# A two-layer decoder trunk: the row of reciprocal norms by two float32r products, a whole copy of the low-rank block, and 32 columns more in the planner's product estimate

## The chip, the cores and the metric

The kernel runs on one core of one Trainium2 chip. The metric is the device time of one execution in microseconds; before the change it is 489.7 us, the median of three runs that lie between 489.56 and 489.83 us. The engines are called as the profile calls them: PE (TensorE's products) and PEld (its weight loads), DVE (VectorE), ACT (ScalarE), POOL (GpSimd) and SP (SyncE, which issues transfers).

## The reference

Two layers of a decoder trunk on 512 tokens of width 1024, all in float32. Cut to what matters:

```python
def hybrid_layer(x, ...):
    h = rmsnorm(x, norm_g)                       # (512, 1024)
    p = h @ w_in                                 # (512, 3488), split by columns
    cq, ckv, kr, g_a, c_h, c_b, c_c, g_b, sg_u, sg_v, g_c, mq, mk, mv, g_d = split(p)
    # A: latent attention, 4 heads. The low-rank block is cq (256), ckv (128), kr (32)
    q  = rmsnorm(cq, mla_q_norm_g) @ mla_w_uq
    kv = rmsnorm(ckv, mla_kv_norm_g) @ mla_w_ukv
    k_rope = rope(rmsnorm(kr, mla_k_rope_g))
    o_a = causal softmax attention on q, [k_nope, k_rope], v
    o_b = c_b * short_conv(c_c * c_h)            # B
    o_c = sg_u * (causal mixing of layernorm(sg_v))   # C
    o_d = attention in blocks, 4 heads, on mq, mk, mv   # D
    y = concat(o_a * silu(g_a), o_b * silu(g_b), o_c * silu(g_c), o_d * silu(g_d))
    return y @ w_out
x = x + hybrid_layer(x, ...)                     # twice
```

## The kernel before

**Products.** Each float32 operand of a large product is split into a high and a low float32r part, and each product is done as three float32r products (high by high, high by low, low by high) that add up in one PSUM bank; `mm3` writes these three. `ScalarE` usually makes a high part (`whi_...`, `hTh...`, `cTh`, `ph..`) and VectorE the low part (`wlo_...`, `hTl`, `cTl`, `pl..`). Transposes and one more product, the one this change is about, run in float32. Some of the large products are made in the seven-product form of Strassen and Winograd (`t1` to `t4`, `p1` to `p4`, `b11` and so on), whose sums of weights are made by accumulating transfers on POOL's queue (`t_sums`, from `TS0` on).

**The planner.** No loop of the kernel fixes the order of the instructions. Every chain of work is a Python generator, and `Order.run` resumes them by due time and priority. It keeps a time `now`, which is the planned time of PE, and a clock for each of ACT (`A`), VectorE (`V`), POOL (`G`) and the transfers (`D`). `Chain.pe` puts a product into PE's queue once its inputs are due (plus `PEMARGIN`, 80 ns) and moves `now` by the estimate that it is given, which is `cost(n)` for a product of n columns. `Chain.act`, `Chain.dve` and `Chain.pool` move their engine's clock by an estimate from the size. Choices between ACT and VectorE (the copies `ct`, the scaling of the softmax rows `pa` and `pd`, the high parts of weights, the means by head) go by whose clock is behind. So each engine gets one fixed order of instructions, and at run time it waits only where a semaphore makes it wait. Some chains start at written times: the mixing of group C at `MIXT`, the row of norms at `ROWT`, the columns of gains at `COLT`, the sums of weights at `TS0`, all in planned nanoseconds.

**Banks and buffers.** PSUM's eight banks are handed out by three sets of slots: `accS` (three, for the large products), `trS` (two, for transposes) and `sS` (three). A slot that nobody has put back makes the chain that wants it wait in the plan, and makes the instruction wait at run time. `t2S` hands out eleven SBUF buffers of 128x512.

**The start of layer 0.** The rows of x are not normalized before the first product. x is transposed (`xT`), split (`hTh`, `hTl`) and multiplied as it is, and the reciprocal norm, rstd, is put in afterwards. `x_stats` gathers the mean squares; at `ROWT` POOL raises them to the power -1/2 into `xv[:, RR, :]`, 128 partitions by four token blocks. Groups whose products come out with the features on the partitions need rstd along a row: `x_row` makes a 128x512 matrix `rd` of four diagonals on POOL, multiplies ones by it in float32 on PE (`rrow`), and ACT writes half of the row and its square to `rh`, which the gates and the convolution read later.

**The low-rank block.** `c_first` makes the products `cq0` to `cq3` of the four token blocks, 416 columns each, in the three `accS` banks and one `sS` bank. For each block `low_chain` copies the first 384 columns to `ct`, transposes them (`cT`), splits the transpose (`cTh`, `cTl`) and makes `q` and `kv`. Beside it `low_stats` takes three sums of squares and a copy of the last 32 columns (`krt`) from the same bank. The bank is put back when both are done, that is after five reads, and the next large products (`sq`, columns of `sg_v` and `mq`) take these banks. In layer 1 the same two functions run on blocks that take the three `accS` banks in turn.

**The heads.** For each head of groups A and D: scores (`sa..`, `sd..`), one pass on VectorE that scales and masks a block and finds its extreme (`pa..`, `pd..`), exponentials on ACT, a reciprocal of the four sums (`mna`, `mnd`), a scaling of each block on ACT or VectorE, transposes on PE (`pTa`, `pTd`), a split (`ph..`, `pl..`) and the products with the values (`oa`, `od`). PE fills the time between these steps with the large products of the groups.

The lines of the profile carry helpers' lines: L178 is the line where `Chain._emit` issues (all of ACT's, VectorE's and POOL's planned instructions), L208 is the line where `Chain.pe` issues. So groups are told apart by the names of their tiles.

Of the kernel before, what the change touches and what calls it, by code (L numbers as in the profile page):

```python
# [11 lines left out]
F32 = mybir.dt.float32  # L12
F32R = mybir.dt.float32r
I32 = mybir.dt.int32
AF = mybir.ActivationFunctionType
ALU = mybir.AluOpType
AX = mybir.AxisListType

P = 128
S = 512  # L20
NT = S // P
# [11 lines left out]
WSLACK = 0.0  # L33
AHEAD, URGENT, VSLACK = 4, 2, 300.0
NWARM, FILL, FILLEND = 6, 0.9, 15000.0
MIXT, MIXLAG, ROWT, COLT = 42000.0, 2000.0, 36000.0, 17500.0
KSPLIT, HMEAN = 6, 0.0
PAIRS = {}
LOPRIO = -5
# [8 lines left out]
SEQ1 = ['p11', 'ga0', 'p21', 'p3', 'ga1', 'p4', 'p2', 'ch0', 'p1', 'p22', 'cc0', 'gd0', 'gd1', 'su0', 'gc0', 'cb0', 'gb0', 'ch1', 'cc1', 'cb1', 'gb1', 'su1', 'gc1']  # L48
K0, K1, KK = (2, 3, 0, 1), (4, 5, 6, 7), (0, 2, 3, 1)
ZPROD = ("b11", "t3", "b21", "t4", "t2", "t1", "b22")  # L50
TS0 = 62000.0
TAIL = ((0, 256), (256, 512))

C_CQ, C_KV, C_GA, C_CH, C_CB, C_CC, C_GB = 0, 256, 416, 672, 928, 1184, 1440
# [96 lines left out]
def run_now(gen):  # L151

    try:
        next(gen)
    except StopIteration as e:
        return [e.value]
# [57 lines left out]


def cost(n):
    return max(n / 2.4, 107.0) + 2.0


@with_exitstack  # L220
def hybrid_trunk(ctx: ExitStack, tc: tile.TileContext, x, positions, norm_g, w_c, w_f, w_t, w_o, mla_q_norm_g,
# [3 lines left out]
    V, A, G, PE = nc.vector, nc.scalar, nc.gpsimd, nc.tensor  # L225

    cst = ctx.enter_context(tc.tile_pool(name="cst", bufs=1))
# [14 lines left out]
    o = Order()  # L242
# [5 lines left out]
    t2S = Slots(o, NT2, lambda name, dt=F32: t2p.tile([P, S], dt, tag="t2", name=name))  # L248
# [254 lines left out]
    def shared(slots, n):  # L503

        left = [n]

        def put(ch):
            left[0] -= 1
            if left[0] == 0:
                slots.put(ch)  # L510
        return put
# [4 lines left out]
    ident = cst.tile([P, P], F32, name="ident")  # L516
# [21 lines left out]
    one_box = run_now(zzS.get(Chain(o), "ones", F32R))  # L538
# [137 lines left out]
    for l in range(DEPTH):  # L676
        L = Layer()
# [38 lines left out]
    def pow_rstd(ch, dst, src, n):  # L716
        return ch.pow(G.tensor_tensor, dst, src, nhalf[:, :n], op=ALU.pow)
# [5 lines left out]
    xhi, xlo = ([Event() for _ in range(KT)] for _ in range(2))  # L723
    xsum = cst.tile([P, NT, KT // 2], F32, name="xsum")
    xv = cst.tile([P, 4, NT], F32, name="xv")
    v_ev, r_ev, rh_ev = Event(), Event(), Event()
    rh_box, rh_put = [], shared(hS, 14)
    RV, RR, RE, REE = range(4)

    def rv(i, t):  # L730
        return xv[:, i, t:t + 1]
# [33 lines left out]
    def x_stats():  # L765
        ch = Chain(o)
        for kp in range(KT // 2):
            yield from ch.wait(xk_ev[2 * kp + 1])
            for t in range(NT):
                yield from ch.act(A.activation, junk[:, 0:2 * P], xk[kp][:, t, :], AF.Square, scale=D ** -0.5,  # L770
                                  accum_out=xsum[:, t, kp:kp + 1])
            c2 = Chain(o, ch.t)
            yield from c2.wait(xk_tr[2 * kp + 1])
            v4S.put(c2)
        yield from ch.dve(V.tensor_reduce, xv[:, RV, :], xsum, axis=AX.X, op=ALU.add)
        yield from ch.dve(V.tensor_scalar, xv[:, RV, :], xv[:, RV, :], 1.0, EPS, op0=ALU.mult, op1=ALU.add)
        t0 = ch.t
        for i, f in ((RE, EPS), (REE, EPS * EPS)):
            yield from ch.dve(V.tensor_scalar, xv[:, i, :], xv[:, RV, :], f, None, op0=ALU.mult)
        o.set(v_ev, ch.t)  # L780
        c2 = Chain(o, max(t0, ROWT))
        yield from pow_rstd(c2, xv[:, RR, :], xv[:, RV, :], NT)
        o.set(r_ev, c2.t)

    def x_row():

        ch = Chain(o)
        yield from ch.wait(r_ev)
        d = yield from t2S.get(ch, "rd")
        yield from ch.pool(G.tensor_tensor, d.rearrange("p (t c) -> p t c", t=NT),  # L790
                           ident.unsqueeze(1).to_broadcast([P, NT, P]),
                           xv[:, RR, :].unsqueeze(2).to_broadcast([P, NT, P]), op=ALU.mult)
        tp = yield from trS.get(ch, "rrow")
        yield from ch.pe(4 * cost(S), PE.matmul, tp, one_box[0][:, 0:P].bitcast(F32), d, start=True, stop=True)
        zz_put(ch)
        t2S.put(ch)
        rh_box.append((yield from hS.get(ch, "rh")))
        yield from ch.act(A.activation, rh_box[0][:, 0:S], tp, AF.Copy, scale=0.5)
        yield from ch.act(A.activation, rh_box[0][:, S:2 * S], tp, AF.Square, scale=0.5)
        trS.put(ch)  # L800
        o.set(rh_ev, ch.t)
# [149 lines left out]


    def low_stats(L, t, a, t0, done):
        ch = Chain(o, t0)
        ssq, krt = L.ssq, L.krt
        ct = L.ct[t]
        for i, (c0, c1) in enumerate(((384, 416), (256, 384), (0, 256))):
            yield from ch.act(A.activation, junk[:, :c1 - c0], a[:, c0:c1], AF.Square, scale=(c1 - c0) ** -0.5,
                              accum_out=ssq[:, t, 2 - i:3 - i])
        yield from ch.act(A.activation, krt[:, t, :], a[:, 384:416], AF.Copy)  # L960
        done(ch)
        m = sm.tile([P, 8], F32, tag="ms", name=f"ms{t}_{L.l}")
        e1, e2 = EPS, EPS * EPS
        if L.l == 0:
            yield from ch.wait(v_ev)
            e1, e2 = rv(RE, t), rv(REE, t)
        yield from ch.dve(V.tensor_scalar, m[:, 0:2], ssq[:, t, 1:3], 1.0, e1, op0=ALU.mult, op1=ALU.add)
        yield from ch.dve(V.tensor_scalar, L.e2[:, t, :], ssq[:, t, 0:2], EPS, e2, op0=ALU.mult, op1=ALU.add)
        yield from pow_rstd(ch, m[:, 4:6], m[:, 0:2], 2)
        L.ms[t] = m  # L970
        o.set(L.stat[t], ch.t)
        yield from ch.dve(V.scalar_tensor_tensor, krt[:, t, :], in0=krt[:, t, :], scalar=m[:, 5:6], in1=L.gr,
                          op0=ALU.mult, op1=ALU.mult)
        L.kr_left -= 1
        if L.kr_left:
            return
        yield from ch.wait(rope_ev)
        yield from rope(ch, krt, 16, cosT, sinT, f"k{L.l}")
        yield from ch.wait(L.QK_ev)
        yield from ch.pool(G.tensor_copy, L.K[:, :, :, 64:96], krt.unsqueeze(2).to_broadcast([P, NT, 4, 32]))  # L980
        o.set(L.kr_ev, ch.t)

    def low_chain(L, t, a, t0, slots):
        ch = Chain(o, t0)
        l = L.l
        done = shared(slots, 2)
        ct = yield from t2S.get(ch, f"ct{t}_{l}")
        L.ct[t] = ct
        o.spawn(low_stats(L, t, a, t0, done))
        if o.clk["A"] < o.clk["V"]:  # L990
            yield from ch.act(A.activation, ct[:, :384], a[:, :384], AF.Copy)
        else:
            yield from ch.dve(V.tensor_copy, ct[:, :384], a[:, :384])
        done(ch)
        tp = yield from trS.get(ch, f"cT{t}_{l}")
        for k in range(3):
            yield from ch.pe(109.0, PE.transpose, tp[:, k * P:(k + 1) * P], ct[:, k * P:(k + 1) * P], ident)
        t2S.put(ch)
        c_h = yield from t2S.get(ch, f"cTh{t}_{l}", F32R)
        c_l = yield from t2S.get(ch, f"cTl{t}_{l}", F32R)  # L1000
        yield from split2(ch, c_h[:, :384], c_l[:, :384], tp[:, :384])
        trS.put(ch)
        q_ps = yield from sS.get(ch, f"q{t}_{l}")
        for k in range(2):
            uq_h, uq_l = yield from unit(ch, f"uq_{l}", k)
            yield from mm3(ch, 384, q_ps[:, :384], c_h[:, k * P:(k + 1) * P], c_l[:, k * P:(k + 1) * P],
                           uq_h[:, k, :], uq_l[:, k, :], k == 0, k == 1)
        o.spawn(q_chain(L, t, q_ps, ch.t))
        uk_h, uk_l = yield from unit(ch, f"ukv_{l}")
        kv_ps = yield from sS.get(ch, f"kv{t}_{l}")  # L1010
        yield from mm3(ch, 512, kv_ps, c_h[:, 256:384], c_l[:, 256:384], uk_h[:, 0, :], uk_l[:, 0, :], True, True)
        t2S.put(ch)
        t2S.put(ch)
        L.up_left -= 1
        if L.up_left == 0:
            units[f"uq_{l}"].slots.put(ch)
            units[f"ukv_{l}"].slots.put(ch)
        yield from kv_chain(L, t, kv_ps, ch.t)
# [668 lines left out]
    def main():  # L1687
        m = Chain(o)
# [207 lines left out]
        early_put(m)  # L1896
        for L in layers:
            l = L.l
            L.ct, L.ms, L.up_left = {}, {}, NT
            L.kr_ev, L.kr_left = Event(), NT  # L1900
            L.vn_alloc = Event()
            L.md_alloc = {"mq": Event(), "mk": Event()}
# [5 lines left out]
            for t in L.torder if l else ():  # L1908
                a = yield from accS.get(m, f"cq{t}_{l}")
# [10 lines left out]
            for n in SEQ1 if L.stok else SEQ:  # L1920
# [6 lines left out]
                elif n in TOKS:  # L1927
                    us = []
                    for ts in PAIRS.get((n, l), range(NT)):
                        ts = ts if isinstance(ts, tuple) else (ts,)  # L1930
                        a = {}
# [15 lines left out]
                else:  # L1947
                    a = yield from accS.get(m, f"{n}_{l}")
# [60 lines left out]
    def start():  # L2009
# [5 lines left out]
        wp = yield from sS.get(cw, "warm")  # L2015
        ones = one_box[0][:, 0:P].bitcast(F32)
        V.memset(ones, 1.0)
        A.activation(xsum[:, 0, 0:1], ones[:, 0:1], AF.Square, scale=D ** -0.5)
        o.fill = lambda: PE.matmul(wp[:, 0:P], ones, ones, start=True, stop=True)
        for _ in range(NWARM):  # L2020
# [29 lines left out]
        o.spawn(main(), None, 10)  # L2050
    o.spawn(t_sums((0, z_src, "t", "b"), *((l, p_src, "p", "p") for l in STOK)), TS0, 4)
    o.spawn(start())
# [51 lines left out]
```

## Time and profile before

| | |
|---|---|
| median of three runs | 489.7 us |
| lowest, highest | 489.56, 489.83 us |
| the profiled execution | 489.73 us |
| its span, first to last instruction | 488.0 us |
| PE busy | 481.6 us, 99% of the span |
| DVE busy | 400.9 us, 82% |
| ACT busy | 329.9 us, 68% |
| POOL busy | 104.4 us, 21% |
| granted PE clock | 0.999 |

The 1.7 us between the span and the time of the same execution lie around the first and the last instruction. PE is busy in nearly all of the span, and its granted clock is full, so the time is read as PE's work plus the places where PE waits. A record of PE has a start and a modelled end, and the ends overlap the next starts; what a product takes from PE is read from one start to the next.

### The profile page before, as it was taken

How to read it: one execution, taken by the hardware profiler on the slowest of the kernel's cores; microseconds unless marked ns; L12 is line 12 of the kernel's file. 1: busy time of each engine (PE TensorE's matmuls, PEld its weight loads, DVE VectorE, ACT ScalarE, POOL GpSimd, SP SyncE). 2: the span in 40 equal slices, each digit the busy share in tenths (PEclk: the TensorE clock that was granted, in tenths of full speed). 3: DMA queues.
4: the chain of work that ended last, by engine and by line, in shares of the span. 5: the costliest groups of instructions: out<-in, count | busy, mean ns of one | idle time of the engine just before them, and what ended most of it. 6: DMA issues, size and time to landing. Idle time of an engine off the chain costs nothing.

```text
span 488.0 us, 7509 instructions
## 1 busy us (share of the span) xinstructions
PE 481.6 (99%) x2432; PEld 408.9 (84%) x2432; DVE 400.9 (82%) x893; ACT 329.9 (68%) x898; POOL 104.4 (21%) x172
## 2 busy tenths in 40 slices
PE   9999999999999999999999999999999999999997
PEld 7988888888887888888889988888888888888786
DVE  3698487668987899789998688979788998997993
ACT  5896837677546766457667788769675687666650
POOL 7855330710051210000031013620402200000000
PEclk9999999999999999999999999999999999999999
DMA  8742335897499888596574186786832744427762
GB/s 263 249 135 78 124 128 218 225 197 162 151 330 240 208 217 218 188 343 224 199 239 145 65 290 250 165 246 177 209 131 85 153 136 146 173 66 258 253 242 89
DMA packets 41904, 92.89 MB, mean 190 GB/s; under 512 B 7158, under 2 KB 23048, under 8 KB 41480
## 3 DMA queue, kind: packets, MB, share of 16 engines
q1 hardware_dynamic: 29168, 79.82, 47.3%
q0 software_dynamic: 12672, 12.58, 16.7%
q8 instruction: 19, 0.31, 0.2%
q14 instruction: 21, 0.17, 0.1%
q10 hardware_dynamic: 24, 0.01, 0.0%
HBM read 84.53 MB, written 33.03 MB: 241 GB/s over the span
## 4 chain that ended last, share of the span: by engine, by line
PE 91%; DVE 3%; ACT 2%; DMA 2%; SPq 1%; issue 1%; ACTq 0%
PE oy L208 6%; PE cq L208 6%; PE kv L208 6%; PE gb L208 5%; PE su L208 5%; PE cc L208 5%; PE sq L208 5%; PE gc L208 5%; PE ch L208 5%; PE ga L208 4%; PE oz L208 4%; PE cb L208 4%; PE py L208 3%; PE ox L208 3%; PE sa L208 3%; PE gd L208 3%
## 5 line engine op out<-in xcount | busy, mean ns | idle before, releaser
L178 ACT ACTIVATE pa<-pa,mna 128x128 f32<-128x128 f32 (+3 forms) x53 | 27.8, 554 | 5.6 <-DVE mna L178 5.5
L178 ACT ACTIVATE pd<-pd,mnd 128x384 f32<-128x384 f32 (+3 forms) x49 | 25.8, 548 | 3.2 <-DVE mnd L178 2.9
L178 ACT ACTIVATE pha<-pTa 128x512 fp32r<-128x512 f32 (+3 forms) x32 | 13.9, 434 | 20.6 <-PE pTa L208 20.4
L178 ACT ACTIVATE phd<-pTd 128x512 fp32r<-128x512 f32 (+3 forms) x32 | 13.8, 434 | 16.1 <-PE pTd L208 15.9
L178 DVE CUSTOM_DVE_ANT_0 pa<-sa,maskb,rs_q 128x512 f32<-128x512 f32 (+3 forms) x32 | 16.6, 544 | 6.2 <-PE sa L208 3.2
L178 DVE TENSOR_TENSOR wlo_p<-raw_p,whi_p 128x512 fp32r<-128x512 f32 x28 | 19.1, 698 | 2.7 <-ACT whi_p L178 2.6
L178 ACT ACTIVATE whi_t<-raw_t 128x512 fp32r<-128x512 f32 x31 | 18.2, 619 | 4.5 <-DMA raw_t<-t 4.5
L208 PE MATMUL cq<-whi_c,hTh 128*128 128x416 f32 x64 | 20.8, 370 | 0.0
L178 DVE TENSOR_TENSOR wlo_t<-raw_t,whi_t 128x512 fp32r<-128x512 f32 x32 | 20.7, 679 | 0.0
L208 PE MATMUL cq<-wlo_c,hTh 128*128 128x416 f32 x64 | 20.0, 359 | 0.0
L178 DVE TENSOR_TENSOR pla<-pTa,pha 128x512 fp32r<-128x512 f32 (+3 forms) x32 | 15.4, 485 | 5.6 <-ACT pha L178 5.6
L208 PE MATMUL cq<-whi_c,hTl 128*128 128x416 f32 x64 | 19.8, 355 | 0.0
L178 POOL TENSOR_TENSOR rs_mk<-rs_mk,nhalf 128x16 f32<-128x16 f32 x2 | 6.5, 3243 | 56.3 <-DVE rs_mk L178 56.3
L178 DVE CUSTOM_DVE_ANT_0 pd<-sd,maskb,rs_mq 128x512 f32<-128x512 f32 (+3 forms) x32 | 17.0, 545 | 1.6 <-PE pTd L208 1.0
L178 DVE TENSOR_TENSOR pld<-pTd,phd 128x512 fp32r<-128x512 f32 (+3 forms) x32 | 15.1, 485 | 3.1 <-ACT phd L178 3.0
L178 POOL TENSOR_SCALAR xss<-xss 128x1 f32<-128x1 f32 x4 | 2.7, 668 | 69.6 <-ACT jk L178 65.3
L372 POOL DMA_DIRECT2D t<-in_w_o_dram x16 | 17.0, 1341 | 2.4 <-DMA t<-t 2.3
L178 DVE TENSOR_TENSOR wlo_b<-raw_b,whi_b 128x512 fp32r<-128x512 f32 x24 | 16.0, 682 | 0.1
L178 ACT ACTIVATE whi_b<-raw_b 128x512 fp32r<-128x512 f32 x23 | 13.9, 622 | 3.1 <-DMA raw_b<-in_w_o_dram 3.0
L178 ACT ACTIVATE whi_p<-raw_p 128x512 fp32r<-128x512 f32 x22 | 13.2, 625 | 3.9 <-DMA raw_p<-in_w_t_dram 3.9
L208 PE MATMUL pTd<-ident,pd 128*128 128x128 f32 x80 | 14.1, 272 | 0.6 <-ACT pd L178 0.6
L208 PE MATMUL pTa<-ident,pa 128*128 128x128 f32 x80 | 14.0, 273 | 0.0
(473 smaller groups left out, 1846.8 us busy)
## 6 DMA issues: line engine op xcount, KB each, us to landing
t<-in_w_o_dram POOLq DMA_DIRECT2D x16, 512.0 KB, 8.3
raw_t<-t SPq DMA_DIRECT2D x16, 512.0 KB, 4.0
raw_b<-in_w_o_dram SPq DMA_DIRECT2D x12, 512.0 KB, 4.0
t<-in_w_o_dram SPq DMA_DIRECT2D x8, 512.0 KB, 4.9
p<-in_w_t_dram POOLq DMA_DIRECT2D x8, 512.0 KB, 14.0
t<-t SPq DMA_DIRECT2D x8, 512.0 KB, 4.7
raw_p<-p SPq DMA_DIRECT2D x8, 512.0 KB, 3.2
ys<-ysc SPq DMA_DIRECT2D x14, 256.0 KB, 5.0
```

What stands on the lines that cost most here:

```text
L178: f(*a, **k)
L208: f(*a, **k)
L372: nc.gpsimd.dma_start(src(l, n, j), src(l, y, j), accum_op=ALU.add, max_dma_last_dim=1024)
```

## The change

1. **The row.** rstd is split on VectorE into a float32r part and the rest (`xr2`), POOL makes two matrices of diagonals (`rdh`, `rdl`, each in a buffer of `t2S`), and PE makes the row by two float32r products that add up in one bank. A float32r copy of the ones is made at the start on VectorE.
2. **The whole copy.** `low_chain` copies all 416 columns of a block to `ct` and puts the bank back at once; the squares, the last 32 columns and the transposes read `ct`. The copy of the 32 columns on ACT is gone, the scaling into `krt` reads `ct`. `low_stats` starts when the copy is done, and `ct` is put back when the transposes and the scaling are done.
3. **The estimate.** `cost(n)` goes from n / 2.4 + 2 ns (at least 109) to (n + 32) / 2.4 ns (at least 108): for 512 columns from 215.3 to 226.7 ns. Since every order is made from these estimates, the order on all engines changes. The written times are moved: `MIXT` from 42 to 44 us, `ROWT` from 36 to 37.7 us, `COLT` from 17.5 to 18 us, `TS0` from 62 to 65 us. These four are due times, not estimates.

```diff
-MIXT, MIXLAG, ROWT, COLT = 42000.0, 2000.0, 36000.0, 17500.0
+MIXT, MIXLAG, ROWT, COLT = 44000.0, 2000.0, 37700.0, 18000.0
-TS0 = 62000.0
+TS0 = 65000.0
 def cost(n):
-    return max(n / 2.4, 107.0) + 2.0
+    return max((n + 32) / 2.4, 108.0)

+    xr2 = cst.tile([P, 2, NT], F32R, name="xr2")
...
         yield from pow_rstd(c2, xv[:, RR, :], xv[:, RV, :], NT)
+        yield from c2.dve(V.tensor_copy, xr2[:, 0, :], xv[:, RR, :])
+        yield from c2.dve(V.tensor_tensor, xr2[:, 1, :], xv[:, RR, :], xr2[:, 0, :].bitcast(F32), op=ALU.subtract)
         o.set(r_ev, c2.t)

     def x_row():
...
-        d = yield from t2S.get(ch, "rd")
-        yield from ch.pool(G.tensor_tensor, d.rearrange("p (t c) -> p t c", t=NT),
-                           ident.unsqueeze(1).to_broadcast([P, NT, P]),
-                           xv[:, RR, :].unsqueeze(2).to_broadcast([P, NT, P]), op=ALU.mult)
+        d = []
+        for i, n in enumerate("hl"):
+            d.append((yield from t2S.get(ch, f"rd{n}", F32R)))
+            yield from ch.pool(G.tensor_tensor, d[i].rearrange("p (t c) -> p t c", t=NT),
+                               ident.unsqueeze(1).to_broadcast([P, NT, P]),
+                               xr2[:, i, :].bitcast(F32).unsqueeze(2).to_broadcast([P, NT, P]), op=ALU.mult)
         tp = yield from trS.get(ch, "rrow")
-        yield from ch.pe(4 * cost(S), PE.matmul, tp, one_box[0][:, 0:P].bitcast(F32), d, start=True, stop=True)
+        for i in range(2):
+            yield from ch.pe(cost(S), PE.matmul, tp, one_box[0][:, P:2 * P], d[i], start=i == 0, stop=i == 1)
         zz_put(ch)
+        t2S.put(ch)
         t2S.put(ch)

     def low_stats(L, t, a, t0, done):
         ch = Chain(o, t0)
         ssq, krt = L.ssq, L.krt
-        ct = L.ct[t]
         for i, (c0, c1) in enumerate(((384, 416), (256, 384), (0, 256))):
             yield from ch.act(A.activation, junk[:, :c1 - c0], a[:, c0:c1], AF.Square, scale=(c1 - c0) ** -0.5,
                               accum_out=ssq[:, t, 2 - i:3 - i])
-        yield from ch.act(A.activation, krt[:, t, :], a[:, 384:416], AF.Copy)
-        done(ch)
...
-        yield from ch.dve(V.scalar_tensor_tensor, krt[:, t, :], in0=krt[:, t, :], scalar=m[:, 5:6], in1=L.gr,
+        yield from ch.dve(V.scalar_tensor_tensor, krt[:, t, :], in0=a[:, 384:416], scalar=m[:, 5:6], in1=L.gr,
                           op0=ALU.mult, op1=ALU.mult)
+        done(ch)

     def low_chain(L, t, a, t0, slots):
         ch = Chain(o, t0)
-        done = shared(slots, 2)
+        done = shared(t2S, 2)
         ct = yield from t2S.get(ch, f"ct{t}_{l}")
-        L.ct[t] = ct
-        o.spawn(low_stats(L, t, a, t0, done))
         if o.clk["A"] < o.clk["V"]:
-            yield from ch.act(A.activation, ct[:, :384], a[:, :384], AF.Copy)
+            yield from ch.act(A.activation, ct[:, :416], a[:, :416], AF.Copy)
         else:
-            yield from ch.dve(V.tensor_copy, ct[:, :384], a[:, :384])
-        done(ch)
+            yield from ch.dve(V.tensor_copy, ct[:, :416], a[:, :416])
+        slots.put(ch)
+        o.spawn(low_stats(L, t, ct, ch.t, done))
         tp = yield from trS.get(ch, f"cT{t}_{l}")
...
-        t2S.put(ch)
+        done(ch)
...
         V.memset(ones, 1.0)
+        V.tensor_copy(one_box[0][:, P:2 * P], ones)
```

More of the change, by code (lines that the diff above doesn't have):

```diff
@@ L1898, in main @@
             l = L.l
-            L.ct, L.ms, L.up_left = {}, {}, NT
+            L.ms, L.up_left = {}, NT
             L.kr_ev, L.kr_left = Event(), NT
```

## The prediction

> **What bounds the kernel now.** I read the page first (busy time, then the chain that ended last), then PE's waits, then the stretches of PE's timeline where the change works.
>
> ```profile
> span 488.0 us, 7509 instructions
> PE 481.6 (99%) x2432; PEld 408.9 (84%) x2432; DVE 400.9 (82%) x893; ACT 329.9 (68%) x898; POOL 104.4 (21%) x172
> PE 91%; DVE 3%; ACT 2%; DMA 2%; SPq 1%; issue 1%; ACTq 0%
> ```
>
> PE is busy in 481.6 of 488.0 us and makes 91% of the chain. So an edit is worth what it takes from PE's own work, and what it takes from or adds to PE's waits; work on ACT, DVE and POOL counts only where PE waits for it. PE's waits are few:
>
> ```profile
> PE warm L2019 <- DVE ones L2017: 1.1, 1, 1.1
> PE pTd L208 <- ACT pd L178: 0.6, 1, 0.6
> PE sq L208 <- ACT krt L178: 0.6, 1, 0.6
> PE gd L208 <- DVE zz L178: 0.3, 1, 0.3
> PE oz L208 <- DVE wlo_b L178: 0.3, 1, 0.3
> ```
>
> Behind the start there are four, 1.8 us in all. That is nearly all that a better order could win; what a worse one could lose has no such limit. The second sum is the spacing of products, from the chain of waits in order of time (start, length, what):
>
> ```profile
> 462.64 5.44 PE ox L208 x24
> ```
>
> 24 products of 512 columns in 5.44 us are 0.2267 us each, which is 544 / 2.4 ns: the new estimate to the digit, and 11 ns above the old one.
>
> **The row.** The sum is made against the profiled execution, 489.73 us (488.0 of span and 1.73 around it); the median of the three runs is 489.70, so a result stands for both. PE's timeline (start, length, instruction):
>
> ```profile
> 44.77 0.39 PE L208 MATMUL sq<-yTh,hTl 128*128 128x512 f32 x1
> 45.00 1.02 PE L208 MATMUL rrow<-rd,ones 128*128 128x512 f32 x2
> 45.46 0.80 PE L208 MATMUL sq<-yTh,hTh 128*128 128x512 f32 x1
> 46.10 0.40 PE L208 MATMUL sq<-yTl,hTh 128*128 128x512 f32 x1
> 46.33 0.40 PE L208 MATMUL sq<-yTh,hTl 128*128 128x512 f32 x1
> ```
>
> From the start of rrow (45.00) to the second product behind it (46.10) are 1.10 us; one ordinary product of these takes 0.23, so the row takes 0.87. Two float32r products take 2 x 0.227 = 0.45 if their weight loads hide as others' do. **-0.42 us**, all on PE's path. The bounds are -0.42 and, if one load stands bare, about -0.2 (a load of this row takes 0.19 us, below).
>
> What the row adds lies elsewhere:
>
> ```profile
> L208 PEld LDWEIGHTS rrow<-rd,ones x2: 187/188/188, 44.8 to 45.0; 128*128 128x128 f32 x2
> L178 POOL TENSOR_TENSOR rd<-ident,xv x1: 1192/1192/1192, 39.7 to 39.7; 128x512 f32<-128x512 f32 x1
> L178 DVE TENSOR_TENSOR th_ga<-ga,rh x2: 690/691/692, 66.5 to 71.9; 128x512 f32<-128x512 f32 x2
> 27.28 0.17 DVE L178 TENSOR_SCALAR xv<-xv 128x4 f32<-128x4 f32 x1
> 38.59 1.00 POOL L178 TENSOR_TENSOR xv<-xv,nhalf 128x4 f32<-128x4 f32 x1
> 39.28 2.13 DVE L178 TENSOR_TENSOR wlo_ga<-raw_ga,whi_ga 128x512 fp32r<-128x512 f32 x2
> 44.97 0.27 POOL L178 TENSOR_SCALAR bmv<-bmv,xv 128x1 f32<-128x1 f32 x1 [4.11 <-DVE krt L178]
> 72.59 0.70 PE mp L208 x6
> ```
>
> POOL makes a second 1.19 us diagonal, DVE two operations of the size of the row at 27.28 (0.17 us), and the copy of ones at the start runs while PE waits for x. In the new order rrow stands 6 us of PE work later than before, so `rh` is there near 53 us; its first reader runs at 66.5. Cover is 13 us: nothing. On DVE the first operation waits for POOL's power, with the weight splits of `ga` queued behind it; the power ends at 39.6 and that operation stands behind a split of `ga`, which ran until 41.4. On POOL the second diagonal holds up the first work on `bmv` (44.97), whose result PE needs in `mp` at 72.59. Nothing for both, and their own 1.2 us if that cover were gone.
>
> **The whole copy.** PE, ACT and DVE around the first bank that is given back:
>
> ```profile
> 29.07 0.35 PE L208 MATMUL cq<-whi_c,hTl 128*128 128x416 f32 x1
> 29.26 0.43 PE L208 MATMUL q<-whi_uq,cTh 128*128 128x384 f32 x1
> 29.53 0.34 PE L208 MATMUL q<-wlo_uq,cTh 128*128 128x384 f32 x1
> 29.84 0.44 PE L208 MATMUL q<-whi_uq,cTl 128*128 128x384 f32 x1
> 30.12 0.34 PE L208 MATMUL q<-whi_uq,cTh 128*128 128x384 f32 x1
> 30.30 0.34 PE L208 MATMUL q<-wlo_uq,cTh 128*128 128x384 f32 x1
> 30.65 0.49 PE L208 MATMUL cT<-ident,ct 128*128 128x128 f32 x3
> 31.74 0.50 PE L208 MATMUL sq<-yTh,hTh 128*128 128x512 f32 x1 [0.60 <-ACT krt L178]
> 26.27 0.55 DVE L178 COPY ct<-cq 128x384 f32<-128x384 f32 x1
> 28.72 0.86 ACT L178 ACTIVATE cTh<-cT 128x384 fp32r<-128x384 f32 x2
> 29.23 0.56 DVE L178 TENSOR_TENSOR cTl<-cT,cTh 128x384 fp32r<-128x384 f32 x1 [0.34 <-ACT cTh L178]
> 31.48 0.21 ACT L178 ACTIVATE krt<-cq 128x32 f32<-128x32 f32 x1
> ```
>
> At 31.74 `sq` waits 0.60 us for ACT's little copy `krt`, the fifth reader of the bank; the copy `ct` had read it by 26.82. With the copy as the only reader the bank is free 4.3 us before `sq` wants it (31.14), and in the new order `sq` comes behind three `kv` and six more `q` products. **-0.60 us.** The same rows show a smaller hold: the first two `q` products take 0.27 and 0.31 us where the fourth takes 0.18 (30.12 to 30.30), because `cTh` starts at 28.72 and `cTl` ends at 29.79. In ACT's new order one square of this block's columns stands ahead of `cTh0`, not three, so it starts some tenths earlier, and `cTl0` with it. 0.09 + 0.13 us go: **-0.22 us**; the bounds are -0.22 and 0.
>
> ACT loses eight `krt` copies; `ct` grows by 32 columns. Both are off PE's path. What could be late instead is a `t2S` buffer, because `ct` is now held until the scaling: the new order has `q3` at 33.1 us of PE work, before at 35.1, so it is not held up in the plan.
>
> **The estimate.** I counted the instruction orders of both builds. The products are the same ones, so PE's own work changes by the row alone. What moves is how much PE work covers each chain. Between the last score product of the first head of D in layer 0 and the first transposes of its weights stand 24 products of 512 columns and six score products before, 15 and the same six after: nine fewer, 9 x 0.227 = 2.04 us less cover, and 15 x 0.227 + (544 + 416 + 288) x 2 / 2.4 ns = 4.4 us left. Other heads move alike, and heads finish earlier: the last head's products with the values stood among `oz` products before, and stand ahead of them all now. Hence DVE is clear of the head sooner, and I take the `oz` wait as gone: **-0.30 us** (bounds -0.3 and 0). The `pTd` wait has this history:
>
> ```profile
> 155.02 0.63 ACT L178 ACTIVATE whi_cc<-raw_cc 128x512 fp32r<-128x512 f32 x1 [2.69 <-DMA raw_cc<-in_w_f_dram]
> 156.07 1.91 ACT L178 ACTIVATE pd<-pd,mnd 128x128 f32<-128x128 f32 x4
> 158.04 0.55 PE L208 MATMUL pTd<-ident,pd 128*128 128x128 f32 x3 [0.60 <-ACT pd L178]
> ```
>
> ACT's queue is in order; it stood 2.69 us at a weight half whose transfer had not landed, and the four scalings behind it came late. Such a hold can be anywhere after a new order. In the new one two of these scalings are on DVE and no weight half stands between the exponentials and the scalings, but one stands between the first and second exponential. So I keep `pd` and `zz` (0.6 + 0.3) as a price that some place will pay: zero change, with bounds -0.9 and +2.04 (the same hold with the cover that is gone).
>
> The Trainium skill, "TensorE: Matmul & The Clock Gate", section "Wait — 56ns, not 53.3ns?", gives a warm start-to-start of N / 2.4 plus some 2.5 ns, 215.7 ns at 512 columns; that is the old estimate, and by it the new one would be too long. The trace disagrees with 226.7 ns, every product here having a weight load of its own.
>
> Sum: 489.73 - 0.42 - 0.60 - 0.22 - 0.30 = 488.19: **488.2 us**.
>
> **Rivals.** A measurement of this kernel tells 0.2% from no change, 0.98 us: faster is below 488.7, slower above 490.7.
>
> (a) One deep hold. A late landing catches one head as it did, now with 2.04 us less cover: the row, `sq` and `q` stay won, `oz` does not: 489.73 - 1.24 + 2.04 = 490.5. For it speaks the row at 155.02; against it that the chain itself is short (pass, exponential, reciprocal and two scalings: five steps of 0.48 us, a fourth of the row at 156.07, are 2.4 us) against the 4.4 us that are left.
>
> (b) Slower: two deep holds. The place is ACT's queue at the heads of D, where weight halves stand among the exponentials; each catch costs 0.60 + 2.04 = 2.64. It decides when a landing is later than the spare 2.0 us in two of the 16 heads: 490.5 + 2.6 = 493.1. For it: DVE is near full in the heads' stages, so a chain that slips isn't made up:
>
> ```profile
> 66.00:198.00 132.00, 131.40 (x687) 111.17 (x686) 107.31 (x249) 85.81 (x215) 25.01 (x23) 1.00 0.85 218
> 325.00:447.00 122.00, 121.65 (x645) 102.74 (x644) 107.37 (x256) 87.47 (x224) 16.31 (x16) 1.00 0.51 147
> ```
>
> (columns: stretch, length, busy time of PE, PEld, DVE, ACT, POOL, clock, share and GB/s of DMA). DVE is busy for 81% and 88%. Against it: PE waited for 0.35 and 0.60 us there in 254 us.
>
> (c) Small holds return the gain. Shorter cover everywhere costs some tenths in five or six places, as `gd` (0.3) shows the size: three more such waits bring 489.1, and no measurable change.
>
> (d) The estimate is wrong for PE at run time, and 215.7 ns is right: PE would run 11 ns per product ahead of the plan, 0.16 us over the 15 products that cover the head, with 16 heads 2.6 us: 490.8. The 5.44 us for 24 products speak against it; a fiftieth.
>
> **How the numbers follow.** Forecast 0.58, (a) 0.12, (b) 0.15, (c) 0.13, (d) 0.02. Faster 0.58; within 0.2% (a) and (c), 0.25; slower (b) and (d), 0.17. The range begins where the 0.9 us of the two waits go as well, 488.2 - 0.9 = 487.3, and ends at (a)'s 490.5; what is left out is (b), (d) and a few per cent below.
>
> **What would show it.** In the profile after: no wait of `sq` for `krt`, or for any reader of a bank; two `rrow` products 0.23 us apart; `q` products 0.17 to 0.18 apart; heads of D ending before `oz` begins; PE's waits behind the start at 1 us or less. I am wrong if PE waits for `pd`, `pa`, `pld` or `pla` in several places, if the wait of an ACT instruction for a `raw_` transfer stands just before such a place, or if `cT` or `q` wait for a `t2S` buffer.

## The result: 8 us slower

The changed kernel takes 498.0 us (median of four runs, 496.6 to 498.1), the kernel before on the same chip 489.8 us (489.6 to 490.0). The ratio is 1.0159, with an interval of 1.0141 to 1.0178. The forecast was 488.2 us, its range ended at 490.5 us, and its rival on the slower side was 493.1 us.

The profiled execution took 498.03 us, 496.3 of them span. The page after the change (span, PE's busy time, the chain that ended last):

```profile
span 496.3 us, 7498 instructions
...
PE 484.7 (98%) x2432; PEld 407.8 (82%) x2432; DVE 402.8 (81%) x901; ACT 328.7 (66%) x897; POOL 106.3 (21%) x173
...
PE 65%; DVE 14%; DMA 12%; ACT 4%; issue 2%; POOL 1%; SPq 1%; ACTq 0%; DVEq 0%; POOLq 0%
```

PE makes 65% of the chain, not 91%; DVE went from 3% to 14% and transfers from 2% to 12%. The number of products is the same, and so is the clock. PE's idle time is 496.3 - 484.7 = 11.6 us where it was 6.4; the other 3.1 us are in its busy time, where a wait that is shorter than the modelled end of the product before leaves no gap. PE's waits:

```profile
PE mixT L208 <- DVE pla L178: 1.2, 1, 1.2
PE warm L2026 <- DVE ones L2023: 1.1, 1, 1.1
PE sd L208 <- ACT mk0d L178: 0.8, 1, 0.8
PE sa L208 <- DVE lo1a L178: 0.8, 1, 0.8
PE tmkd L208 <- DVE mk L178: 0.8, 1, 0.8
PE oy L208 <- DVE xr L178: 0.7, 1, 0.7
PE oz L208 <- DVE wlo_b L178: 0.6, 1, 0.6
PE py L208 <- DVE x L178: 0.6, 1, 0.6
```

Besides the start there are eleven waits, 6.7 us in all (four smaller ones aren't shown), where there were four, 1.8 us. They lie at eleven different places. Behind PE, the instructions of DVE that wait for a transfer:

```profile
DVE yaa L178 <- DMA ysc<-yaa: 4.0, 2, 2.4
DVE ys L178 <- DMA ys<-ysc: 3.1, 3, 1.4
DVE whi_p L178 <- DMA raw_p<-p: 3.0, 1, 3.0
```

The same of ACT, its two longest:

```profile
ACT whi_t L178 <- DMA raw_t<-t: 10.4, 8, 3.8
ACT whi_b L178 <- DMA raw_b<-in_w_o_dram: 8.8, 5, 3.6
```

DVE stands 10.1 us at transfers, 4.0 of them at writes of y to its scratch in DRAM (`ysc`), whose buffer it wants again; it stood 2.7 us before. ACT stood 4.5 us before at `raw_t` and 3.0 at `raw_b`. The landings themselves moved with the order. Of the loads of `raw_p`, the first line is before, the second after (transfers, size, median us from issue to landing; one landing is known in each):

```profile
raw_p<-p SPq DMA_DIRECT2D x8, 512.0 KB, 3.2
raw_p<-p SPq DMA_DIRECT2D x8, 512.0 KB, 7.1
```

Before, that load was issued at 308.1 us, 1.1 us ahead of the next group of accumulating transfers; after, at 310.9, 3.9 us behind the first of them. The chain between 115 and 161 us shows how such a wait reaches PE (start, length, what):

```profile
115.32 4.36 DMA ysc<-yaa
...
119.77 0.68 DVE yaa L178
120.45 0.60 DVE wlo_cc L178
121.05 0.60 DVE u L178
121.66 0.61 DVE pla L178
...
122.31 0.66 PE mixT L208 x4
...
135.94 7.64 DMA raw_gb<-in_w_f_dram
...
143.60 0.63 ACT whi_gb L178
144.23 1.48 ACT pd L178 x6
...
150.79 1.21 DVE wlo_gb L178 x2
...
152.07 7.32 DMA raw_cc<-in_w_f_dram
...
159.41 0.04 ACT whi_cc L178
...
160.07 0.69 ACT mk0d L178
...
160.80 1.21 PE sd L208 x5
```

Read from the bottom: `sd` waits for `mk0d` on ACT; `mk0d` stands in ACT's queue behind the weight half `whi_cc`; that stands at the transfer of `raw_cc`, which was issued only when DVE had split the weight before (`wlo_gb`); and that ran late, behind a head's exponentials on ACT and DVE's own queue, because the earlier transfer, `raw_gb`, had landed 7.64 us after its issue. So one late landing makes the next load late. In the tail it is a write and a read back that set the end:

```profile
455.42 6.42 DMA ysc<-yad
...
461.89 2.65 DMA ys<-ysc
...
481.42 8.47 PE oy L208 x36
```

Between the last two rows the chain runs on DVE; it comes back to PE only at 481.4 us.

### The profile page after: what moved, and what is told of

Its sections match the earlier page's. It is cut to its first block, busy times and chain, and to the rows that moved or that the text cites. A ratio compares the mean times of both kernels' runs of the same rounds, so it can differ in the third digit from the quotient of the medians.

```text
span 496.3 us, 7498 instructions
## 1 busy us (share of the span) xinstructions
PE 484.7 (98%) x2432; PEld 407.8 (82%) x2432; DVE 402.8 (81%) x901; ACT 328.7 (66%) x897; POOL 106.3 (21%) x173
## 4 chain that ended last, share of the span: by engine, by line
PE 65%; DVE 14%; DMA 12%; ACT 4%; issue 2%; POOL 1%; SPq 1%; ACTq 0%; DVEq 0%; POOLq 0%
PE cq L208 7%; PE kv L208 6%; PE oy L208 5%; PE gb L208 4%; PE ga L208 4%; PE sq L208 4%; PE cb L208 3%; PE cc L208 3%; PE ch L208 3%; DMA ysc<-yaa 2%; PE pz L208 2%; PE sa L208 2%; PE od L208 2%; PE sd L208 2%; PE pTd L208 2%
## 5 line engine op out<-in xcount | busy, mean ns | idle before, releaser
L178 ACT ACTIVATE pa<-pa,mna 128x256 f32<-128x256 f32 (+3 forms) x46 | 24.3, 551 | 2.6 <-DVE mna L178 2.6
L178 ACT ACTIVATE whi_t<-raw_t 128x512 fp32r<-128x512 f32 x31 | 18.6, 623 | 10.4 <-DMA raw_t<-t 10.4
L178 POOL TENSOR_TENSOR rs_mq<-rs_mq,nhalf 128x16 f32<-128x16 f32 x2 | 6.8, 3398 | 49.4 <-DVE rs_mq L178 49.4
L178 ACT ACTIVATE whi_p<-raw_p 128x512 fp32r<-128x512 f32 x24 | 14.5, 621 | 2.5 <-DMA raw_p<-p 2.5
```

Source lines behind the costliest of these rows:

```text
L178: f(*a, **k)
```

## The experiments

Ratios are to the kernel before, on the same chip.

### One part at a time

```diff
 e1_row       : the row's lines of the change; cost, times and low_chain as before
 e2_copy      : low_chain and low_stats of the change; the rest as before
 e4_row_copy  : both
 e3_est       : the rest as before
-    return max(n / 2.4, 107.0) + 2.0
+    return max((n + 32) / 2.4, 108.0)
```

> Before with the row alone (two float32r products; old estimate, old due times, bank held for five reads). The first theory, the estimate: the longer estimate makes a plan with shorter covers, PE then waits in many places and the tail falls behind DVE; without it the row keeps its gain, 489.8 - 0.4 = 489.3 us, between 489.0 and 489.8. The second theory, any new order: the order of before is a favourable one, the row's two planned products instead of four move `now` by 0.4 us and every later choice with it, and PE pays some us of new waits: 491 to 496 us. The third theory, the due times (the sums of weights and the mixing start 2 to 3 us later, transfers land later): no due time is moved here, so 489.3 us.

> Before with the whole copy alone. The first theory (the estimate) and the third (the due times): the wait of `sq` for `krt` (0.60 us) and the slow `q` products (0.22 us) go, 489.8 - 0.8 = 489.0 us. The second theory (any new order): 491 to 496 us, with new waits of PE at `pd`, `pa`, `mk` or `lo` like those after the change.

> Before with the estimate alone, (n + 32) / 2.4, the due times as before. The first theory: most of the loss is here, 489.8 + 8.2 + 1.2 (the row and the copy do not save here) less what the due times add: 495 to 499 us, with six or more waits of PE behind the start. The third theory: the due times are not moved, so 490 us. The second theory: 491 to 498, no nearer to the changed kernel than the row or the copy alone.

> Before with the row and the whole copy, the estimate and the due times as before. The first theory: 489.8 - 0.42 - 0.60 - 0.22 = 488.6 us, the gain of the prediction without its estimate. The second theory: 491 to 496 us. The third theory: 488.6 us.

Measured: the row 0.9982 (0.9968 to 0.9996), the copy 1.0045 (1.0023 to 1.0067), the estimate 1.0016 (1.0005 to 1.0027), row and copy 1.0072 (1.0051 to 1.0093). The row gains about what its sum says (its trace also lacks the wait of `pTd`, so not all of it need be the row's own). The first theory, that the estimate itself loses, falls: alone it costs 0.8 us, not 5 to 9. The copy was to gain 0.8 us and loses 2.2. Its profile has no wait of `sq` for `krt`, as expected; the waits of PE it has instead:

```profile
PE sd L208 <- DVE mnd L178: 2.1, 1, 2.1
PE py L208 <- ACT hi0a L178: 1.8, 1, 1.8
```

The first, at 157.5 us, lies more than 100 us behind what the copy touches in layer 0, the second, at 334.1, more than 40 us behind what it touches in layer 1. What the copy does there is to change the order.

### The due times and the old estimate

```diff
 e7_after_old_times, the changed kernel with
-MIXT, MIXLAG, ROWT, COLT = 44000.0, 2000.0, 37700.0, 18000.0
+MIXT, MIXLAG, ROWT, COLT = 42000.0, 2000.0, 36000.0, 17500.0
-TS0 = 65000.0
+TS0 = 62000.0
 e9_old_estimate, the changed kernel with
-    return max((n + 32) / 2.4, 108.0)
+    return max(n / 2.4, 107.0) + 2.0
```

> The changed kernel with the four due times of before (MIXT, ROWT, COLT, TS0). The first theory, the estimate: its loss is all here, 496 to 499 us. The second theory, any new order: one more order among many; row with copy gave a ratio of 1.0072 and the estimate 1.0016, so it lies anywhere from 490 to 497. The third theory, the due times: without them the loss is that of row and copy and estimate alone, 490 x 1.0072 x 1.0016, some 494 us, and the other 4 us come from the moved times.

> The changed kernel with the estimate of before, n / 2.4 + 2 (row, whole copy and the four moved due times stay). The first theory: the loss goes, 489 to 491 us. The second theory: anywhere from 490 to 497. The third theory: the moved times keep their 4 us on top of the 3.5 us of row and copy, some 497 us.

Measured: 1.0153 (1.0096 to 1.0211) with the old times, 1.0012 (0.9996 to 1.0027) with the old estimate. The third theory falls: the moved times cost nothing that can be seen under the new estimate (its interval is wide), and under the old one they bring row and copy from 1.0072 to 1.0012. Effects that add up don't behave so; orders that are drawn anew do. These two runs by themselves would also fit the first theory; the runs with 16 and 31 columns, next, don't.

### A step of 0.4 ns

```diff
 the changed kernel with 16, 30, 31 and 33 for 32
-    return max((n + 32) / 2.4, 108.0)
+    return max((n + 31) / 2.4, 108.0)
```

> The changed kernel with 16 columns in the estimate, (n + 16) / 2.4: 220.0 ns for 512 columns, half way between the two estimates. The first theory (the estimate itself: longer products in the plan, shorter covers): half way, 490 x 1.008 = 494 us. The second theory (an order is a draw among many): anywhere from 490 to 498, with no place on a line.

> The changed kernel with 30 columns in the estimate, 225.8 ns for 512 columns; with 31 the ratio was 0.9983, with 32 1.0159, with 33 1.0222, with 16 1.0151. The theory of a draw: anywhere from 488 to 501 us, nearer to 496 than to 489 as most draws were. If there is a region of good estimates below 31: 489 to 490 us.

> The changed kernel with 31 columns in the estimate: 226.25 ns for 512 columns, 0.4 ns under the changed kernel's 226.67, and under 0.2% of a product. The first theory: the covers are the same, so the time is that of the changed kernel, 496.5 to 499 us. The second theory: the order is another draw, and the time differs by 2 us or more.

> The changed kernel with 33 columns in the estimate, 227.08 ns for 512 columns. The first theory: 496.5 to 499 us, as with 31. The second theory: another draw; this and the run with 31 columns differ from each other and from the changed kernel by 2 us or more.

| columns added | ratio | interval |
|---|---|---|
| 16 | 1.0151 | 1.0113 to 1.0190 |
| 30 | 1.0049 | 1.0032 to 1.0065 |
| 31 | 0.9983 | 0.9968 to 0.9999 |
| 32 (the change) | 1.0159 | 1.0141 to 1.0178 |
| 33 | 1.0222 | 1.0177 to 1.0267 |

One column is 0.42 ns per product, and between 31 and 33 lie 11 us. There is no line through these points, and neither neighbour of 31 columns is as good as it is. (With 30 the time is 492.0 us: not the 489 to 490 of a good region, but nearer to that than the theory of a draw leaned.) Compared place by place in the two traces, 1,191 of the 2,432 places in PE's order hold another product with 31 columns than with 32. PE's two longest waits with 31, behind the start:

```profile
PE py L208 <- DVE x L178: 1.1, 1, 1.1
PE cq L208 <- ACT hTh L178: 1.0, 2, 0.7
```

Late landings are here too: that load of `raw_p` takes 7.9 us, and DVE stands 3.8 us at it. But ACT stands 5.0 us at `raw_t`, not 10.4, and DVE nowhere at a write to the scratch. That less of what PE needs soon stands behind late landings in this order is argued from this, not shown.

The same step on the kernel before:

```diff
 e18_before_plus and e19_before_minus
-    return max(n / 2.4, 107.0) + 2.0
+    return max(n / 2.4, 107.0) + 2.4
 (+ 1.6 in the other)
```

> The kernel before with its estimate 0.4 ns longer for every product, n / 2.4 + 2.4, nothing else. If the order of before is a favourable draw, a step of 0.4 ns loses as the change did: 491 to 498 us. If its neighbours are as good, 489.5 to 490.5 us.

> The kernel before with its estimate 0.4 ns shorter, n / 2.4 + 1.6, nothing else. If the order of before is a favourable draw: 491 to 498 us. If its neighbours are as good: 489.5 to 490.5 us.

Measured: 1.0067 (1.0051 to 1.0083) with 0.4 ns more, 1.0002 (0.9986 to 1.0019) with 0.4 ns less. One neighbour loses and one is as good, so neither expectation holds for both: before is as good as the better of its two neighbours, and a step of 0.4 ns and nothing else can cost 3.2 us.

### Without the transfers, in the same order

```diff
 e10_after_no_sums, e11_before_no_sums, e17_cols33_no_sums
-                nc.sync.dma_start(src(l, n, j), src(l, x, j))
+                pass
-                nc.gpsimd.dma_start(src(l, n, j), src(l, y, j), accum_op=ALU.add, max_dma_last_dim=1024)
+                pass
 e16_no_sums_no_scratch (after), e20_before_no_sums_no_scratch: besides
-                nc.sync.dma_start(ysc[L.l][kt], yv)
+                pass
-            dma(c2, P * 2048, w[-1], ysc[L.l][kt])
+            dma(c2, P * 2048, w[-1], w_t[0, 0, kt % 4][:, 0:S])
...  (in all five, z_src and p_src name plain weights of the same size)
```

> The changed kernel without the transfers that make the sums of weights (the copies on SP's queue and the accumulating ones on POOL's); the weights t1 to t4 and p1 to p4 are read from plain weights of the same size, so the sums are left out and the output differs. The orders of PE, DVE and ACT are those of the changed kernel. If PE's new waits come from loads and writes that land late beside the sums (each of the seven larger waits follows back to a transfer of 3.7 to 7.6 us), they go and the time falls by 4 to 8 us, to 489 to 494 us. If they come from covers that are too short by themselves, PE waits as before and the time stays over 496 us.

> The kernel before without the same transfers (sums left out, output differs); the orders of PE, DVE and ACT are those of before. Its waits of PE behind the start are 1.8 us, so at most that goes: 488 to 489.8 us by every theory. It is the measure for the run beside it: if late transfers are the channel, the difference of the two is under 2 us, if covers are, it stays near 7 us.

> The changed kernel without the sums of weights (as in the run before) and without the writes of y to its scratch in DRAM; the later reads take as many bytes from a weight instead, so they wait for no write. The output differs; the orders of PE, DVE and ACT are those of the changed kernel. Without the sums alone the ratio was 1.0032, with PE waits at `mixT` (1.3), `oz` (0.9), `oy` (0.7) and `py` (0.6), and DVE standing 4.8 us at the scratch. If queues that stand at transfers are the whole channel, these go as well and the time is that of the kernel before without sums or up to 1 us above it: 489.0 to 490.3 us. If covers too short by themselves hold the rest, it stays at 491.5 to 492.5 us.

> The kernel before without the sums of weights and without the writes of y to the scratch (both left out, the output differs; the reads take weights of the same size); the orders of PE, DVE and ACT are those of before. It closes the account: the changed kernel without them is at 0.9978. If the loss goes wholly through transfers, what is left between the two is the gain of the row and of the bank given back early, 1.0 us by the sum (0.42 + 0.60), less the changed kernel's remaining waits: before comes out at 0.997 to 0.9985, 488.3 to 489.0 us, within 1 us of the changed one. If a loss by short covers remains, before is at 0.995 or less.

> The worst order so far (33 columns, 500.5 us) without the sums of weights (left out, output differs); the orders of PE, DVE and ACT are those of the kernel with 33 columns. If late landings beside the sums are the channel in this order too, it falls by 5 us or more, to 490 to 495 us, and the half clock after its long waits is gone. If the order is bad by itself, it stays above 497 us.

| | before | after |
|---|---|---|
| whole | 1 | 1.0159 (1.0141 to 1.0178) |
| without sums | 0.9975 (0.9961 to 0.9988) | 1.0032 (1.0021 to 1.0043) |
| without sums and scratch writes | 0.9990 (0.9979 to 1.0002) | 0.9978 (0.9965 to 0.9990) |

Each column has one order of PE, DVE and ACT throughout; the traces show the same instructions in the same places. The distance falls from 1.6% to 0.57% (1.0032 / 0.9975) without the sums, and to -0.12% (0.9978 / 0.9990) without the scratch writes: 5 of the 8 us go with the sums, the other 3 with the scratch. Without the sums it is 2.8 us, a little over the 2 us that late transfers were given and far under the 7 of short covers. Without both, the two kernels come out at 488.7 and 489.2 us, a little under and a little over what was expected of them. The last -0.12% is in the direction of the row's and the copy's own gain, but smaller than the 1.0 us worked out, and its two intervals overlap. So little, about 1 us at most within these intervals, is left for covers that are too short where nothing lands late. The changed kernel without both, the page's chain:

```profile
PE 91%; DVE 3%; DMA 3%; ACT 1%; SPq 1%; issue 1%; ACTq 0%; DVEq 0%
```

Its waits of PE behind the start, the three longest:

```profile
PE oz L208 <- DVE wlo_b L178: 0.9, 1, 0.9
PE py L208 <- DVE x L178: 0.6, 1, 0.6
PE kv L208 <- ACT Q L178: 0.2, 1, 0.2
```

And the tail of its chain in order of time:

```profile
447.81 4.31 PE oz L208 x19
452.12 5.44 PE ox L208 x24
457.56 5.44 PE oz L208 x24
463.00 5.44 PE ox L208 x24
468.44 13.83 PE oy L208 x60
```

The waits at `mixT`, `sd`, `sa`, `tmkd` and `oy` are gone, and the tail is PE's own again, with the heads where the changed kernel has them. For these heads the shorter cover was enough by itself. Two waits that were to go as well have stayed. `oz` still goes back to a late landing, of the 6.73 us read that stands in the place of the scratch's. `py` keeps its 0.6 us in every run of this order, and its chain here goes back through DVE's queue to the scores on PE, to no transfer: that cover is too short by itself. With 33 columns and no sums the ratio is 1.0085 (1.0052 to 1.0118) instead of 1.0222: there too most of the loss goes with the sums, and the half clock of its profile (last section) with it; what holds the rest was not separated.

### Planning the landings as they are

```diff
 e15_after_landing, the changed kernel with
-        ch.t = o.clk["D"] + 2000.0
+        ch.t = o.clk["D"] + 4000.0
-                ch.t = max(ch.t, t0 + 3000.0)
+                ch.t = max(ch.t, t0 + 6000.0)
```

> The changed kernel with the plan's landing of a transfer moved from 2 to 4 us behind its estimated end, and the planned end of a write of y to its scratch from 3 to 6 us: a weight half of 512 KB is then planned to land 5.5 us after its issue where the changed kernel's loads take 4.2 to 7.1 us in the median and a scratch write 4.4. If the queues of DVE and ACT stand because the plan takes transfers too short, and the plan now takes them as they are, most of the loss goes: 489.5 to 493 us, and DVE's waits for `raw_p` (3.0 us) and for the scratch writes (4.0 us) go. If it is only another draw, anywhere from 490 to 498 and other waits of DVE and ACT for transfers as large.

Measured: 1.0095 (1.0068 to 1.0121), 494.6 us. It misses the range that it was given. The waits go as expected: DVE stands 1.1 us at `raw_p` and not at all at the scratch writes, ACT 0.6 us at `raw_t` where it stood 10.4. But a new one comes, ahead of layer 1, that no transfer ends:

```profile
PE hT L208 <- ACT a L178: 2.4, 1, 2.4
```

So the order has a hole of its own, as a draw would. With the half clock that follows it (below) it costs some 4.1 us. That the waits for transfers went because the plan took the landings as they are is not shown: the order changed too, and in the changed kernel with the old estimate DVE's waits at `raw_p` and at the scratch writes are gone too.

## Why the prediction was wrong

**What bounds the kernel.** Right as a reading: PE's own work bounds it, and four waits of 1.8 us were nearly all that could be won. "What a worse one could lose has no such limit" stood there too, and was not priced.

**The row, -0.42.** Right. PE's timeline after the change:

```profile
50.69 0.39 PE L208 MATMUL rrow<-rdh,ones 128*128 128x512 f32 x1
50.92 0.39 PE L208 MATMUL rrow<-rdl,ones 128*128 128x512 f32 x1
51.15 0.39 PE L208 MATMUL sq<-yTh,hTh 128*128 128x512 f32 x1
```

Two products, 0.23 us each, with the loads hidden; alone the row gives 0.9982, 0.9 us with an interval of 0.2 to 1.6.

**The whole copy, -0.60 and -0.22.** Right at its place: no `sq` waits for a reader of a bank, and the first `q` products are 0.17 us apart (29.63, 29.80, 29.97). The hold of before was 0.1 us larger than worked out: the third `q` product (29.84 to 30.12) took 0.28 too. One of the `kv` products behind them is late instead (33.56 to 34.09, 0.53 us where 0.23 is usual). Wrong as a price of the edit: alone it loses 2.2 us where 0.8 of gain was worked out, since the new order was counted as free.

**The estimate, -0.30 for `oz`.** Right at its place. The wait of before is in layer 1; there the heads of D now end at 451.8 us, before `oz` begins at 452.7, and no `oz` waits. The `oz` wait of the changed kernel is another one, in layer 0. The first row is before, the second after:

```profile
458.50 0.50 PE L208 MATMUL oz<-wlo_b,yD 128*128 128x512 f32 x1 [0.26 <-DVE wlo_b L178]
225.66 0.50 PE L208 MATMUL oz<-wlo_b,yD 128*128 128x512 f32 x1 [0.63 <-DVE wlo_b L178]
```

**The estimate, zero for the rest.** This is the step that failed: the waits that a new order brings were put at no change. The price of "such a hold" was taken from the one that was seen, 0.60 plus 2.04 us of cover, and kept at zero net; there are eleven waits, 6.7 us, where there were 1.8, besides the shorter ones in PE's busy time. And the argument that the heads of D have 4.4 us of cover against a chain of 2.4 looked at one kind of chain and one queue. Of the seven waits listed above, followed back like those two, one (`sd`) is a catch in ACT's queue at a head of D. Four (`mixT`, `tmkd`, `oz`, `oy`) go back to a write or a read of the scratch through DVE's queue, `tmkd` through two powers on POOL of 3.1 and 3.3 us besides. `sa` goes back to `raw_p` through DVE's queue. `py` stands behind that `sa`, but it has the same 0.6 us where its chain meets no transfer, so its own cover was too short. The signs that the prediction gave came in part: PE waits for `pla` (1.2), `pd` (0.3) and `pa` (0.2), and ACT's wait for `raw_cc` stands just before `sd`. That 0.2267 us is the true spacing was right, and helped nothing. By the plan a load of 512 KB lands 3.5 us behind its issue; those on the chains above took 3.7 to 7.6.

**The rivals.** (b), late landings caught in ACT's queue, named the mechanism; its size was two holds, 3.3 us above before. It lacked that DVE's queue stands as well, that one late landing delays the next load through the two weight buffers, that writes to the scratch catch too, and that in the tail the chain stays on DVE for 17 us. (c), small holds, had the shape, eleven waits of 0.2 to 1.2 us, but priced three more of 0.3 each. (d) was rightly small: products of 512 columns still come 0.23 us apart. Missing was the rival that the plan is drawn anew: of the fourteen plans run here with all their transfers, the changed kernel among them, two are faster than before, two are not told apart from it (e9 and e19) and ten are slower, by 0.16% to 2.2%. As far as these runs show, a good order among them is luck.

**What stays open.** Which of the moved rows decide between 31 and 32 columns was not singled out, nor how much of a loss comes from landings that became later and how much from work that now stands behind them.

## What to carry to other kernels

Where a planner writes the order and choices hang on comparisons of clocks, an edit's price has two parts: its own work, and a new draw of the whole order. The second can be ten times the first (11 us between 31 and 33 columns, against a gain of 1.0 us worked out for the row and the copy), so measure the same edit under a few estimates that differ by a fraction of a nanosecond before saying what it is worth; the row and the copy give 0.9983 under 31 columns and 1.0159 under 32. And look at the landings in the plan before the sizes of products: here most of what PE paid for stood in an in-order queue at a late landing. That a plan with truer landings is faster is not shown; the one that was run took 494.6 us.

## What the runs showed of the hardware

A long wait of PE can cost nearly twice its length. With 33 columns PE waits 1.4 us for `hi1a` and 0.8 us for `lo1a` near 325 us; the stretches there (length, busy time of PE, PEld, DVE, ACT, POOL, granted clock, share and GB/s of DMA):

```profile
324.00:326.00 2.00, 0.50 (x1) 0.19 (x1) 2.00 (x6) 2.00 (x7) 0.00 (x0) 1.00 1.12 334
326.00:328.00 2.00, 1.39 (x4) 1.21 (x5) 1.20 (x4) 1.25 (x8) 0.00 (x0) 0.51 0.39 142
328.00:330.00 2.00, 2.00 (x8) 1.90 (x7) 1.75 (x6) 1.32 (x3) 1.22 (x4) 0.50 0.00 1
330.00:332.00 2.00, 2.00 (x7) 1.52 (x5) 0.00 (x0) 0.69 (x4) 0.91 (x2) 0.50 0.00 0
332.00:334.00 2.00, 2.00 (x13) 1.76 (x13) 1.43 (x6) 1.04 (x4) 0.00 (x0) 0.78 0.00 0
```

PE is busy for 0.50 of the two microseconds from 324 on, and from 326 to nearly 333 its clock is granted at half, so products of 512 columns come 0.43 us apart. In their profiles the copy alone shows the same behind its wait of 2.1 us (half clock from 158.3 to 161.7), row and copy behind one of 1.9 us (333.2 to 336.6), and the changed landings behind the wait of `hT` above (259.8 to 263.2). 3.4 us at half the clock cost a busy PE some 1.7 us, an estimate from these stretches, beside the wait. The changed kernel, whose longest wait is 1.2 us, stays at 1.00, and the wait of 1.8 us at `py` in the copy alone had no half clock behind it. But the length of one wait doesn't decide: with 33 columns the clock falls once more (360.2 to 363.6) behind three waits of 0.5, 0.4 and 0.2 us, and with 16 columns (364.1 to 367.5) behind two of 0.5 and 1.2. Nor does the order alone: of nine executions of the copy alone, four have a mean granted clock of 0.995 to 0.997 (492.7 to 493.8 us) and five of 1.000 (489.2 to 493.0), and with 33 columns the profiled one alone, 503.8 us, has 0.990. In every trace here the changes of the clock lie whole steps of 3.41 us apart; what in a step decides was not found. The Trainium skill, "TensorE: Matmul & The Clock Gate", section "What's actually happening", puts the fall to half behind at least one idle window of about 3.4 us; the length of the half-clock stretches (3.4 us behind a single wait) agrees with such a window, but here waits of 1.9 to 2.4 us were enough, and so were several shorter ones.
